# Per-head products over 64 array rows, with the two heads taken in turn, in a two-layer RWKV-7 / gated-unit trunk

## The chip, the cores and the metric

The program runs on one core of a Trainium2 chip. The core has a matrix engine with a 128 by 128 array (TensorE, PE in the profile; PEld is its weight load), a vector engine (VectorE, DVE), a scalar engine (ScalarE, ACT), GpSimd (POOL) and a queue that issues DMAs (SyncE, SP). Each engine runs its own instructions in the order in which the program holds them and waits on semaphores for the others. The metric is device time of one execution, in microseconds.

## The reference, cut to what matters

The trunk has two layers on 512 tokens of width 1024, and a dense feed-forward part behind each layer. The change touches only the token mixer of layer 0, which carries a state per head (16 heads of 64 channels) through time:

```python
def step(S, inp):
    r_t, w_t, k_t, v_t, a_t, b_t = inp
    sa = jnp.einsum('bhij,bhj->bhi', S, a_t)
    S = (S * w_t[:, :, None, :]
         + sa[..., None] * b_t[:, :, None, :]
         + v_t[..., None] * k_t[:, :, None, :])
    y = jnp.einsum('bhij,bhj->bhi', S, r_t)
    return S, y
```

The kernel does not step through time. It cuts the 512 tokens into 8 chunks of 64. Inside a chunk the recurrence becomes a small triangular system per head, so that each chunk and head needs products of keys with queries (64 by 64 blocks), the inverse of a unit triangular matrix, and products with that inverse. Between chunks only the 64 by 64 state is carried.

## The kernel before, in words

The 16 heads are worked in four blocks of four heads (b = 0 to 3). A block holds two pairs of heads (q = 0, 1), and a pair lies on the 128 partitions: the first head on partitions 0 to 63, the second on 64 to 127. For a block the program has these stages:

- `early`: the projections' results become decays, keys and queries, which are written to DRAM in the layout of the next stage (`sa`, `sb`).
- `front`: loads them back and makes the products of keys with queries. It goes over four units: half of the chunks (`hh`, four chunks each) times pair (`q`). For each unit and each head it fills a PSUM bank `lm` with four products, one per chunk (`cc`), at L709. VectorE multiplies one half of the bank by the causal mask and puts it into `MV` (L712), and ScalarE copies other parts into `LA` and `BX` (L715, L716). Four transposes `bkt` (L722) and their copies end the unit. GpSimd masks one part of `BX` at L717.
- `back`: turns `LA` into the inverse. VectorE eliminates 16 by 16 blocks in 15 steps (`tm`, `Dm`, L744 and L746) between 32 by 32 transposes (`LX`, `hn`, `Dt`), and TensorE joins the blocks (`Qp`, `Np`, `Tp`, `Q2p`, `T2p`), with copies into `bdT` (L783, L802). Then for each unit: `mp` (L807, the inverse times a transposed part of `MV`), a copy, and for each head a bank `gh` with four products (L814), from which VectorE makes the final `MV` with two additions (L816, L817).
- `scan`: runs through the eight chunks with the products `us` (next state) and `Yp` (output), then group norm and gating follow.

`MV` holds for each unit and head a 128-partition slab: the head's own queries in its own 64 partitions. The other 64 partitions are zeroed by GpSimd first (L688), because the `lm` product contracts over all 128 partitions while the weights `ST` hold both heads; later the masked product is written to those other partitions. So an `lm` product contracts over 128 rows, 64 of which multiply zeros. A `gh` product already contracts over one head's 64 partitions (`rows`). All these operands are float32, and each such product stands in the profile as two instructions: a bank of four products is eight rows of the trace.

`lm`, `bkt` and `mvt` take PSUM banks 1 and 2 in turn (tag `pl`), and `gh` takes banks 3 and 4 in turn (tag `pt`). The order of the instructions on every engine is set by the framework's scheduler when the program is built: it interleaves the stages of several blocks (the list `PLAN` gives their priority) with the value projection `v`, which is one long run of products over 128 rows, and with the output projection `acc`. After the mixer come output projection, feed-forward, the gated unit of layer 1 and its feed-forward, all outside the change.

## Time and profile before

| | us |
|---|---|
| median of 3 runs (1423.27 to 1425.45) | 1424.7 |
| the profiled execution, its own time | 1426.41 |
| its span, first to last instruction | 1424.7 |
| TensorE busy | 1338.3 (94%) |
| VectorE busy | 791.8 (56%) |
| ScalarE busy | 569.1 (40%) |
| GpSimd busy | 274.5 (19%) |
| mean granted TensorE clock | 0.962 |
| `lm` products, 256 instructions, TensorE busy | 41.6 |
| `gh` products, 256 instructions, TensorE busy | 33.4 |
| zeroing of `MV` on GpSimd, 32 instructions | 16.6 |

The stages around the change lie between 195 us (first `lm`) and 461 us (last `gh`) from the start of the span. Times in rows of the timeline are start and length in microseconds; a row with x16 holds sixteen instructions that follow each other, and its length reaches from the start of the first to the end of the last. Matmuls overlap in the array's pipeline, so the pace of a run of them is read from the starts of the rows and not from the length of one. In the table by stretches each engine's figure is its busy time, PEclk the granted clock.

### The profile page before, as it was taken

The page shows a single profiled execution, that of the slowest core. Times are in us where ns is not written, and L with a number is a line of the kernel's source. Part 1 is how long each engine was busy: PE and PEld are TensorE (multiplying, and loading weights), DVE is VectorE, ACT ScalarE, POOL GpSimd, SP SyncE. Part 2 cuts the span into 40 slices and gives each one's busy share as a digit, 9 for nine tenths or more (in the row PEclk, how much of TensorE's full clock was granted, in tenths as well). Part 3 has the DMA queues.
Part 4 walks back from the last instruction along what each step waited for, and adds up shares of the span by engine and source line. Part 5 has one row for each costly group of instructions (what it writes and reads, how often), then busy time and mean ns, then how long its engine had stood idle before and what let it go on. Part 6 is the DMA issues. An engine that isn't in the chain of part 4 may idle for free.

```text
span 1424.7 us, 21481 instructions
## 1 busy us (share of the span) xinstructions
PE 1338.3 (94%) x8472; PEld 1091.2 (77%) x8472; DVE 791.8 (56%) x1318; ACT 569.1 (40%) x1060; POOL 274.5 (19%) x248
## 2 busy tenths in 40 slices
PE   5899997987889979999999999999999999999998
PEld 3576686976768768888888888778888888888886
DVE  6962776388685775554544222865575455443223
ACT  5654665363723363323322122743363232322221
POOL 6154463133311231111111000210121111110000
PEclk9999998987969989999999999999999999999999
DMA  5133467351322423333332232343213333332331
GB/s 157 30 107 92 127 182 200 94 150 43 87 65 88 130 90 104 89 89 103 90 99 94 89 118 74 104 129 109 89 52 112 103 89 89 103 90 103 89 96 67
DMA packets 210324, 143.04 MB, mean 100 GB/s; under 512 B 59664, under 2 KB 185136, under 8 KB 210224
## 3 DMA queue, kind: packets, MB, share of 16 engines
q1 hardware_dynamic: 208544, 135.90, 32.2%
q0 software_dynamic: 1680, 5.77, 1.3%
q8 instruction: 67, 1.10, 0.3%
q14 instruction: 33, 0.27, 0.1%
HBM read 125.39 MB, written 14.16 MB: 98 GB/s over the span
## 4 chain that ended last, share of the span: by engine, by line
PE 77%; DVE 7%; ACT 2%; issue 2%; DMA 2%; POOL 1%; SPq 1%; DVEq 0%; POOLq 0%; ACTq 0%
PE gu L158 12%; PE gu L156 12%; PE gu L157 12%; PE acc L156 8%; PE acc L157 8%; PE acc L158 8%; PE gh L814 2%; PE lm L709 2%; PE u L156 1%; PE u L158 1%; PE u L157 1%; PE Yp L856 1%; PE mp L807 1%; PE proj L158 1%; PE proj L156 1%
## 5 line engine op out<-in xcount | busy, mean ns | idle before, releaser
L131 ACT CAST whi<-wraw 128x1024 fp32r<-128x1024 f32 x161 | 168.8, 1050 | 472.5 <-PE gu L157 257.2
L132 DVE TENSOR_TENSOR wlo<-wraw,whi 128x1024 fp32r<-128x1024 f32 x161 | 246.6, 1532 | 197.2 <-ACT whi L131 193.2
L157 PE MATMUL gu<-hT,whi 128*128 128x512 f32 (+1 forms) x768 | 289.6, 378 | 4.4 <-DVE hT L59 4.4
L156 PE MATMUL gu<-hT,whi 128*128 128x512 f32 (+1 forms) x768 | 290.2, 380 | 0.8 <-ACT hT L57 0.8
L158 PE MATMUL gu<-hT,wlo 128*128 128x512 f32 (+1 forms) x768 | 289.7, 378 | 0.0
L157 PEld LDWEIGHTS gu<-hT,whi 128*128 128x128 f32 x768 | 146.0, 190 | 34.0 <-DVE hT L59 4.7
L156 PEld LDWEIGHTS gu<-hT,whi 128*128 128x128 f32 x768 | 145.8, 191 | 29.5 <-ACT hT L57 1.0
L158 PEld LDWEIGHTS gu<-hT,wlo 128*128 128x128 f32 x768 | 145.8, 190 | 29.0 <-issue 0.2
L157 PE MATMUL acc<-wlo,act 128*128 128x512 f32 x416 | 163.9, 394 | 0.0
L156 PE MATMUL acc<-whi,act 128*128 128x512 f32 x416 | 163.6, 394 | 0.0
L158 PE MATMUL acc<-whi,act 128*128 128x512 f32 x416 | 160.5, 394 | 0.0
L333 POOL TENSOR_TENSOR sg<-sg,hn 128x512 f32<-128x512 f32 x44 | 56.7, 1288 | 422.5 <-DVE sg L332 422.5
L332 DVE TENSOR_TENSOR sg<-sg,gu 128x512 f32<-128x512 f32 x44 | 30.2, 687 | 142.5 <-PE gu L158 141.1
L148 POOL TENSOR_TENSOR wlo<-wraw,whi 128x1024 fp32r<-128x1024 f32 x28 | 70.1, 2505 | 169.9 <-ACT whi L147 151.1
L158 PEld LDWEIGHTS acc<-whi,act 128*128 128x128 f32 x416 | 78.2, 188 | 18.1
L156 PEld LDWEIGHTS acc<-whi,act 128*128 128x128 f32 x416 | 78.2, 188 | 18.0
L157 PEld LDWEIGHTS acc<-wlo,act 128*128 128x128 f32 x416 | 78.1, 188 | 18.0
L330 DVE TENSOR_TENSOR sg<-gu,hn 128x512 f32<-128x512 f32 x44 | 30.4, 691 | 67.8 <-PE gu L158 67.6
L131 ACT CAST act<-sg 128x512 fp32r<-128x512 f32 x52 | 32.3, 622 | 72.2 <-POOL sg L333 58.1
L158 PE MATMUL proj<-xsp,wlo 128*128 128x512 f32 x128 | 53.7, 421 | 0.0
L156 PE MATMUL proj<-xsp,whi 128*128 128x512 f32 x128 | 51.9, 405 | 0.4 <-ACT k L529 0.4
L709 PE MATMUL lm<-MV,ST 128*128 128x128 f32 x256 | 41.6, 316 | 11.2 <-DMA ST<-sb 7.9
(305 smaller groups left out, 2248.8 us busy)
## 6 DMA issues: line engine op xcount, KB each, us to landing
wraw<-in_ffn_w_gate_dram SPq DMA_DIRECT2D x44, 512.0 KB, 3.6
wraw<-in_ffn_w_up_dram SPq DMA_DIRECT2D x44, 512.0 KB
wraw<-in_ffn_w_down_dram SPq DMA_DIRECT2D x44, 512.0 KB, 3.6
wraw<-in_rwkv_w_rkv_dram SPq DMA_DIRECT2D x24, 512.0 KB, 3.5
wraw<-in_sgu_w_in_dram SPq DMA_DIRECT2D x16, 512.0 KB, 3.6
x<-in_x_dram SPq DMA_DIRECT2D x8, 512.0 KB, 3.7
MV<-sa SPq DMA_DIRECT2D x64, 64.0 KB, 2.6
ST<-sb SPq DMA_DIRECT2D x8, 512.0 KB, 4.5
```

Source lines behind the costliest of these rows:

```text
L131: self.nc.scalar.copy(hi, src)
L132: self.nc.vector.tensor_tensor(lo, src, hi.bitcast(F32), op=ALU.subtract)
L148: nc.gpsimd.tensor_tensor(lo, raw, hi.bitcast(F32), op=ALU.subtract)
L156: mm(out, lhs[0], rhs[0], start=start, stop=False)
L157: mm(out, lhs[0], rhs[1], start=False, stop=False)
L158: mm(out, lhs[1], rhs[0], start=False, stop=stop)
L330: nc.vector.tensor_tensor(sg, pp[0], yb, op=ALU.mult)
L332: nc.vector.tensor_tensor(sg, sg, pp[1], op=ALU.mult)
L333: nc.gpsimd.tensor_tensor(sg, sg, yb, op=ALU.mult)
L709: mm(lm[:, cc * P:(cc + 1) * P], st[:, cc].rearrange("p n t -> p (n t)"), mv[:, :, cc, hd, :], start=True, stop=True)
L807: mm(mp[:, cc * P:(cc + 1) * P], bdT[:, q * NC + 4 * hh + cc].rearrange("p h t -> p (h t)"), mt[:, cc, :], start=True, stop=True)
L814: mm(gh[:, cc * P:(cc + 1) * P], mt[rows, cc, :], bx[rows, 0:2, cc, :], start=True, stop=True)
```

## The change

The zeroing of the other 64 partitions goes. The `lm` product now takes weights and moving operand from one head's 64 partitions only, as `gh` did before. In the text of the program the loops are turned round: two banks are taken at once, one for each head, and for each chunk the two heads' products follow each other, so that neighbouring products use the array's rows 0 to 63 and 64 to 127 in turn. The same turn is made for `gh`. What is read out of the banks, by whom and in which order of heads, is as before.

```diff
                         mv = MV[hh, q] = s4("MV", [P, 2, 4, 2, C])
                         for hd in range(2):
-                            g.memset(mv[head[1 - hd], :, :, hd], 0.0)
                             for n in range(2):
...
+                    lms = [self.bank("pl", "lm") for _ in range(2)]
+                    for cc in range(4):
+                        for hd in range(2):
+                            mm(lms[hd][:, cc * P:(cc + 1) * P], st[head[hd], cc].rearrange("p n t -> p (n t)"),
+                               mv[head[hd], :, cc, hd, :], start=True, stop=True)
                     for hd in range(2):
                         rows, other = head[hd], head[1 - hd]
-                        lm = self.bank("pl", "lm")
-                        for cc in range(4):
-                            mm(lm[:, cc * P:(cc + 1) * P], st[:, cc].rearrange("p n t -> p (n t)"), mv[:, :, cc, hd, :], start=True, stop=True)
-                        lv = lm.rearrange("p (c a t) -> p c a t", c=4, a=2)
+                        lv = lms[hd].rearrange("p (c a t) -> p c a t", c=4, a=2)
...
+                    ghs = [self.bank("pt", "gh") for _ in range(2)]
+                    for cc in range(4):
+                        for hd in range(2):
+                            mm(ghs[hd][:, cc * P:(cc + 1) * P], mt[head[hd], cc, :], bx[head[hd], 0:2, cc, :], start=True, stop=True)
                     for hd in range(2):
-                        rows, other = head[hd], head[1 - hd]
-                        gh = self.bank("pt", "gh")
-                        for cc in range(4):
-                            mm(gh[:, cc * P:(cc + 1) * P], mt[rows, cc, :], bx[rows, 0:2, cc, :], start=True, stop=True)
-                        gv = gh.rearrange("p (c a t) -> p a c t", c=4, a=2)
+                        gv = ghs[hd].rearrange("p (c a t) -> p a c t", c=4, a=2)
```

The scheduler builds its order anew, and its order is what the engines run. Three places follow. First TensorE in `back` of block 3, at the unit whose bank pair is shown (in the changed kernel `us` is L845, `Yp` L858, `gh` L815, `mp` L809). Before, with the second unit:

```order
L807 MATMUL mp_4530<-MVt_4241,bdT_151 128x128 x4
L856 MATMUL Yp_4703<-su_4692,MV_3207 64x64 x2
L856 MATMUL Yp_4703<-su_4692,MV_3214 64x64 x2
L843 MATMUL us_4798<-su_4790,MV_3476 64x64 x2
L814 MATMUL gh_4536<-BX_3543,MVt_4241 128x128 x4
L814 MATMUL gh_4543<-BX_3543,MVt_4241 128x128 x4
L807 MATMUL mp_4550<-MVt_4254,bdT_151 128x128 x4
```

Changed, the same unit:

```order
L809 MATMUL mp_4498<-MVt_4209,bdT_151 128x128 x4
L858 MATMUL Yp_4671<-su_4660,MV_3187 64x64 x2
L858 MATMUL Yp_4671<-su_4660,MV_3192 64x64 x2
L845 MATMUL us_4766<-su_4758,MV_3452 64x64 x2
L815 MATMUL gh_4504<-BX_3511,MVt_4209 128x128
L815 MATMUL gh_4505<-BX_3511,MVt_4209 128x128
L815 MATMUL gh_4504<-BX_3511,MVt_4209 128x128
```

The two heads' banks (4504 and 4505) are filled in turn. Over all four blocks 10 of the 16 `gh` units stand so in the changed program, 2 still have four products of one head directly followed by four of the other, and 4 have other products between the two heads; before, it was 0, 13 and 3.

Second, TensorE at the end of `front` of block 0 and the beginning of `front` of block 1 (`v` is the value projection). Before:

```order
L722 MATMUL bkt_1598<-ident_79,ST_1492 128x128 x4
L709 MATMUL lm_1610<-MV_1501,ST_1492 128x128 x4
L709 MATMUL lm_1619<-MV_1501,ST_1492 128x128 x4
L722 MATMUL bkt_1629<-ident_79,ST_1492 128x128 x4
L757 MATMUL mvt_1691<-ident_79,MV_1478 128x128 x4
L757 MATMUL mvt_1697<-ident_79,MV_1485 128x128 x4
L757 MATMUL mvt_1704<-ident_79,MV_1494 128x128 x4
L757 MATMUL mvt_1710<-ident_79,MV_1501 128x128 x4
L709 MATMUL lm_2080<-MV_2041,ST_2039 128x128 x4
L709 MATMUL lm_2089<-MV_2041,ST_2039 128x128 x4
L722 MATMUL bkt_2099<-ident_79,ST_2039 128x128 x4
L709 MATMUL lm_2111<-MV_2048,ST_2039 128x128 x4
```

Changed:

```order
L724 MATMUL bkt_1590<-ident_79,ST_1488 128x128 x4
L708 MATMUL lm_1602<-MV_1495,ST_1488 128x128 x4
L708 MATMUL lm_1603<-MV_1495,ST_1488 128x128 x4
L724 MATMUL bkt_1621<-ident_79,ST_1488 128x128 x4
L759 MATMUL mvt_1683<-ident_79,MV_1478 128x128 x4
L759 MATMUL mvt_1689<-ident_79,MV_1483 128x128 x4
L759 MATMUL mvt_1696<-ident_79,MV_1490 128x128 x4
L759 MATMUL mvt_1702<-ident_79,MV_1495 128x128 x4
L156 MATMUL v_2417<-whi_2421,xsp_1431 128x256
L156 MATMUL v_2418<-whi_2421,xsp_1431 128x256
L708 MATMUL lm_2064<-MV_2033,ST_2031 128x128 x4
L708 MATMUL lm_2065<-MV_2033,ST_2031 128x128 x4
```

Here the heads are not taken in turn: bank 1602 gets its four products, then 1603 its four. Of the 16 `lm` units one is fully in turn (the last of block 2), one in part (the first of block 0), 5 have the second half of one head's products directly ahead of the other's, and 9 have other products between the two heads. After the last row shown, 27 products of `v` follow in the changed program before `bkt` and the first head of block 1's second unit, 19 more before its second head, and 29 more before `Qp`; before, the two `lm` units of block 1 stood together and 60 of `v` behind them.

Third, VectorE where block 1's last copy into `bdT` stands among the first steps of block 2's elimination (`Y<-Y` is group norm of block 0; in the changed kernel `tm` is L746, `Dm` L748, the copy L804). Before:

```order
L744 TENSOR_TENSOR tm<-LX,Dm 128x2x48
L885 TENSOR_TENSOR Y<-Y,nr_y 128x1024
L746 TENSOR_TENSOR Dm<-Dm,tm 128x2x12x4
L744 TENSOR_TENSOR tm<-LX,Dm 128x2x55
L746 TENSOR_TENSOR Dm<-Dm,tm 128x2x11x5
L802 COPY bdT<-T2p 32x16x32
```

Changed:

```order
L887 TENSOR_TENSOR Y<-Y,nr_y 128x1024
L714 TENSOR_TENSOR MV<-lm,mk_126 64x4x2x64 x2
L737 STREAM_TRANSPOSE LX<-LA 128x1024
L903 TENSOR_TENSOR Y<-Y,hn 128x1024
L746 TENSOR_TENSOR tm<-LX,Dm 128x2x15
L804 COPY bdT<-T2p 32x16x32
```

The copy, for which `mp` of block 1 waits, has moved from behind the fifth step of block 2's elimination to ahead of the end of its first.

## The prediction

> **What bounds the kernel now.** I read the page first, engine shares and chain, then the stretch of the mixer by windows, then the two groups of products, then single rows of the timeline.

> ```profile
> PE 1338.3 (94%) x8472; PEld 1091.2 (77%) x8472; DVE 791.8 (56%) x1318; ACT 569.1 (40%) x1060; POOL 274.5 (19%) x248
> PE 77%; DVE 7%; ACT 2%; issue 2%; DMA 2%; POOL 1%; SPq 1%; DVEq 0%; POOLq 0%; ACTq 0%
> PE gu L158 12%; PE gu L156 12%; PE gu L157 12%; PE acc L156 8%; PE acc L157 8%; PE acc L158 8%; PE gh L814 2%; PE lm L709 2%; PE u L156 1%; PE u L158 1%; PE u L157 1%; PE Yp L856 1%; PE mp L807 1%; PE proj L158 1%; PE proj L156 1%
> ```

> TensorE carries 77% of the chain that ends last, and `gh` and `lm` 2% each, some 28 us apiece. That share is an average over stages with different limits. The windows cut it (columns: length, busy PE, PEld, DVE, ACT and POOL with instruction counts, granted clock, DMA share, GB/s):

> ```profile
> 195.00:240.00 45.00, 35.03 (x258) 31.48 (x259) 28.96 (x48) 29.25 (x67) 23.55 (x29) 0.86 0.72 188
> 240.00:300.00 60.00, 58.30 (x904) 54.51 (x903) 34.13 (x65) 28.68 (x66) 10.71 (x17) 0.96 0.42 119
> 300.00:345.00 45.00, 31.56 (x600) 27.80 (x601) 37.13 (x76) 21.46 (x60) 16.46 (x20) 0.72 0.30 80
> 345.00:380.00 35.00, 33.98 (x592) 28.68 (x591) 19.45 (x45) 19.88 (x59) 5.45 (x11) 0.97 0.28 67
> 380.00:415.00 35.00, 23.97 (x233) 19.76 (x223) 34.50 (x68) 13.81 (x25) 13.45 (x8) 0.62 0.28 93
> 415.00:440.00 25.00, 23.18 (x516) 19.52 (x516) 10.01 (x23) 10.20 (x25) 0.00 (x0) 0.92 0.18 54
> 440.00:490.00 50.00, 49.49 (x454) 40.46 (x453) 38.33 (x89) 17.87 (x43) 16.24 (x16) 1.00 0.42 131
> ```

> TensorE is full in 240 to 300, 345 to 380 and 440 to 490: there less TensorE work is less time. In 300 to 345 and 380 to 415 VectorE is the busy one (37.1 of 45, 34.5 of 35) and TensorE idles at a low clock, and in 195 to 240 TensorE idles 10 us. The long waits of TensorE between 190 and 490 (total, times, longest):

> ```profile
> PE mp L807 <- DVE bdT L802: 12.8, 3, 7.3
> PE lm L709 <- DMA ST<-sb: 7.9, 2, 4.6
> ```

> **What two halves of the array do at once.** First the two groups (busy us, mean ns of one, idle before), then single runs of them:

> ```profile
> L709 PE MATMUL lm<-MV,ST 128*128 128x128 f32 x256 | 41.6, 316 | 11.2 <-DMA ST<-sb 7.9
> L814 PE MATMUL gh<-BX,MVt 64*128 64x128 f32 x256 | 33.4, 313 | 1.8 <-ACT MVt L809 1.1 <-DVE MV L817 0.7
> ```

> Sixteen instructions are one unit, both heads; eight are one head. At full clock, then at half clock:

> ```profile
> 296.81 2.05 PE L709 MATMUL lm<-MV,ST 128*128 128x128 f32 x16
> 286.35 1.16 PE L709 MATMUL lm<-MV,ST 128*128 128x128 f32 x8
> 287.44 1.71 PE L814 MATMUL gh<-BX,MVt 64*128 64x128 f32 x16
> 456.22 1.16 PE L814 MATMUL gh<-BX,MVt 64*128 64x128 f32 x8
> 232.09 3.76 PE L709 MATMUL lm<-MV,ST 128*128 128x128 f32 x16 [4.63 <-DMA ST<-sb]
> 341.15 3.10 PE L814 MATMUL gh<-BX,MVt 64*128 64x128 f32 x16
> ```

> One head takes 1.16 us over 64 rows as over 128, so halving the rows alone buys nothing. Two heads take 2.05 over 128 rows (0.89 more, 8 steps of 0.11) but 1.71 in `gh`, where they lie on different halves, though one head's eight stand wholly ahead of the other's. So 0.34 us, three steps, already overlap at the change of head. Three windows inside one such unit show it (the count is of instructions that run in the window):

> ```profile
> 269.48:270.02 0.55, 0.54 (x4) 1.00 0.00 0
> 270.02:270.47 0.45, 0.45 (x9) 1.00 0.00 0
> ```

> Twice as many run in the second, shorter window, in which the first head ends and the second begins. Heads in strict turn should then take one head's time, 1.16.

> [...]

> **The change, part by part.** *`gh`.* The new order takes 10 of 16 units in turn: 1.71 becomes 1.16, 0.55 saved, about 1.0 at half clock (3.10 to some 2.1). By blocks: block 0 all four, 2.2 us, in the full stretch 240 to 300. Block 1 three, one of them at half clock, 2.1; between them TensorE also waits for the copy of `mp` and for the additions, so I count half, 1.0. Block 2 one at half clock, 1.0, in the stretch that VectorE fills: 0. Block 3 two, 1.1, but one unit's heads, together before, are now apart, which costs (2 x 1.16 - 1.71) 0.6: 0.5 in a full stretch. Sum 3.7 us on the path, of about 6 on the engine. Bounds: 6 saved; or, if alternate products did not overlap, these ten would cost as `lm` does, 10 x 0.34 = 3.4 slower. The second window makes me take the saving.

> *`lm`.* Only one unit is fully in turn (0.89 saved), five stand head behind head (0.34 each, 1.7), nine have other work between and save nothing. Against that, a product over 64 rows among full ones is a change of the array's shape. The price, from `mp` with the same shape behind it and with another:

> ```profile
> 290.74 1.06 PE L807 MATMUL mp<-MVt,bdT 128*128 128x128 f32 x8
> 291.63 0.60 PE L757 MATMUL mvt<-ident,MV 128*128 128x128 f32 x4
> 450.82 1.16 PE L807 MATMUL mp<-MVt,bdT 128*128 128x128 f32 x8
> 451.91 0.45 PE L856 MATMUL Yp<-su,MV 128*64 128x64 f32 x4
> ```

> Start to start it is 0.89 against 1.09, so 0.1 for each change. In the new order 25 sides of `lm` runs newly border on full products (`v`, `ssp`, `bkt`, `yt`, `mp`), 19 of them before 250 us: 2.5 us in all. So on the engine `lm` is nearly even (2.6 saved, 2.5 paid). What is paid early (1.9 against 0.7 saved there) lies in the stretch with 10 us of idle TensorE, 0; without that cover it would cost 1.2. Later 1.9 is saved, 0.6 paid: 1.3 on the path. Bounds: 14 saved (16 x 0.89) if the hardware brought all heads together; 2.5 lost if none overlap.

> [...]

> *The zeroing.* 32 instructions leave GpSimd:

> ```profile
> L688 POOL MEMSET MV<- 64x512 f32 x32 | 16.6, 520 | 27.6 <-DVE MV L816 20.4 <-PE v L158 3.5 <-PE Yp L856 2.2
> ```

> 16.6 us of an engine that is busy 19% of the span; behind them in its queue stand the masks of `BX` and the memsets of the next stage. The loads of `MV` wait in any case for the slot, and the first `lm` for `ST`'s DMA (7.9 above). I count 0; at most the 3.8 us that weight loads of `lm` waited on these memsets, if the DMA were not as late:

> ```profile
> L709 PEld LDWEIGHTS lm<-MV,ST 128*128 128x128 f32 x256 | 36.6, 221 | 14.5 <-issue 9.2 <-POOL MV L688 3.8 <-POOL hn L899 0.4
> ```

> *Both banks at once.* A unit's first head is now read out only when all eight of its turns are done, 1.16 against 1.16 where they run together, so nothing; where a unit is split over other work, the order shows one head first as before.

> *The new order elsewhere.* Products of `v` move from behind block 1's second `lm` unit into its first idle, and `mp` of block 1 gets its last copy earlier. It can give back at most the waits above (12.8 + 7.9) and can make as many new ones. I take 0 and put both signs into the rivals.

> Sum: 3.7 + 1.3 = 5.0 us. From the profiled span, 1424.7, to 1419.7; the span's 1424.7 is also the median of the runs (the profiled execution as a whole took 1426.4, 1.7 around the span), so I predict 1420 for the median.

> **The rivals.** *More than the sum: the wait of `mp` goes.* In block 1:

> ```profile
> 326.22 1.92 DVE L735 STREAM_TRANSPOSE LX<-LA 128x1024 f32<-128x1024 f32 x1
> 336.68 0.69 DVE L802 COPY bdT<-T2p 32x512 f32<-32x512 f32 x1
> ```

> 10.5 us lie between them; in the new order one group-norm product and one step do, about 3.5, then `T2p` sets the time. If 5 of these 7 us arrive at the scan, 1415. Against it: VectorE has the same total work in 300 to 345, so what is pulled ahead delays block 2's elimination.

> *Slower: block 0's inverse comes late.* Place: `Qp` of block 0, at 249 us now. The first `lm` unit of block 1 waits for its DMA until 232 as today and takes up to 3.1 at half clock; 27 products of `v` at 0.12 (0.24 at half clock), then the unit's heads with 19 and 29 more between and behind. Pace of `v`:

> ```profile
> 204.37 0.28 PE L156 MATMUL v<-whi,xsp 128*128 128x256 f32 x1
> 204.49 0.28 PE L157 MATMUL v<-wlo,xsp 128*128 128x256 f32 x1
> ```

> 232.1 + 3.1 + 3.2 to 6.5 + about 1 for transposes and head + 2.3 + 1 + 3.5 puts `Qp` between 246 and 250.5, and VectorE's elimination waits for the mask of that unit's first head in its own queue. With the shape changes ahead of it (1.9) that is up to 3 us late. If VectorE, which fills 37 of the 45 us behind, passes the delay on and the `gh` savings fall into waits, 1424.7 + 3 = 1428. It decides from a `Qp` later than 250.

> *No change.* VectorE sets the pace in 300 to 345 and 380 to 415, and the savings ahead of each are waited away; or shape changes cost more than 0.1: 1423 to 1426.

> [...]

> **How the numbers follow.** The forecast, 1417 to 1422, 0.37; the earlier copy, 1412 to 1416, 0.15; full overlap 0.05; no change 0.23; slower 0.20. About 0.2% (2.9 us) is what a measurement of this kernel can tell from no change. Faster by more is 0.34 of the forecast's 0.37, and 0.15 and 0.05: 0.54. Within it the 0.23 and the forecast's last 0.03: 0.26. Slower 0.20. The range runs from the earlier copy with all 6 us of `gh` (1424.7 - 6 - 1.3 - 7, about 1410) to the late `Qp` with a microsecond for its own uncertainty, 1429.

> **What would show it.** `gh` units in turn should take 1.16 with 16 instructions, and `lm` head behind head 1.71; the group `lm` should fall from 41.6 by 2 to 3 us at most, `gh` from 33.4 by about 6. `Qp` of block 0 should start within a microsecond or two of 249. The stretches 240 to 300 and 440 to 490 should be shorter by 2 and 0.5. I am wrong if alternate `gh` takes 2.05, or if the last `gh` (460 us) comes more than 10 us earlier or any later.

## The result: slower by 1.2%

The changed kernel takes 1437.74 us in the median of 4 runs (1437.46 to 1449.61), the kernel before 1423.99 on the same chip (4 runs, 1419.73 to 1425.45). The ratio is 1.0119, 95% interval 1.0077 to 1.0162: 13.7 us slower, where 1420 was predicted and 1429 was the upper end of the range. The profiled execution of the changed kernel took 1437.75 us, its span is 1436.0; the profiled execution of the kernel before has a span of 1424.7, so the two that are compared below lie 11.3 us apart.

The page of the changed kernel, engine shares and chain:

```profile
PE 1344.0 (94%) x8472; PEld 1090.3 (76%) x8472; DVE 794.1 (55%) x1318; ACT 569.3 (40%) x1060; POOL 257.8 (18%) x216
PE 77%; DVE 7%; DMA 2%; issue 2%; ACT 2%; SPq 1%; POOL 1%; DVEq 0%; POOLq 0%; ACTq 0%
```

Nothing stands out there. The groups of the two products (busy us, mean ns of one, idle before) show that the products got shorter:

```profile
L708 PE MATMUL lm<-MV,ST 64*128 64x128 f32 x256 | 37.9, 322 | 5.5 <-DMA ST<-sb 2.9 <-ACT BX L718 1.7 <-issue 0.6
L815 PE MATMUL gh<-BX,MVt 64*128 64x128 f32 x256 | 29.0, 313 | 3.8 <-ACT MVt L811 1.9 <-DVE MV L819 1.8
```

Two single units in the timeline (start, length):

```profile
286.10 1.16 PE L815 MATMUL gh<-BX,MVt 64*128 64x128 f32 x16
287.10 1.61 PE L708 MATMUL lm<-MV,ST 64*128 64x128 f32 x16
```

`lm` fell from 41.6 to 37.9 us and `gh` from 33.4 to 29.0; a `gh` unit in turn takes 1.16, and an `lm` unit with one head behind the other 1.61. 8.1 us of products are gone, and TensorE is busy 5.7 us longer, so products run longer somewhere. The stretches say where (length, busy PE, PEld, DVE, ACT, POOL with counts, granted clock, DMA share, GB/s):

```profile
345.00:380.00 35.00, 32.29 (x574) 27.04 (x570) 22.17 (x52) 20.51 (x60) 3.31 (x6) 1.00 0.28 66
380.00:415.00 35.00, 17.43 (x222) 14.48 (x223) 32.68 (x63) 10.59 (x18) 11.67 (x7) 0.60 0.29 88
415.00:440.00 25.00, 25.00 (x261) 21.00 (x260) 8.02 (x20) 7.62 (x18) 0.00 (x0) 0.67 0.18 58
```

From 415 to 440 TensorE is busy all the time and gets through 261 instructions, where it got through 516 before: the clock is 0.67 in place of 0.92. Starts (and ends where named) on TensorE, from the timelines, in us:

| | before | changed | difference |
|---|---|---|---|
| `Qp` block 0 | 249.4 | 251.0 | +1.6 |
| `T2p` block 0 | 260.7 | 267.9 | +7.2 |
| `Qp` block 2 | 360.3 | 359.9 | -0.4 |
| `T2p` block 2 | 388.5 | 394.6 | +6.1 |
| first `mp` block 2 | 397.0 | 401.7 | +4.7 |
| `Qp` block 3 | 424.9 | 435.2 | +10.3 |
| end of the last `gh` | 461.5 | 472.2 | +10.7 |
| end of the mixer's last `acc` | 510.2 | 521.7 | +11.5 |

The 7 us that block 0 loses are back by 360 us. Nearly all of the loss, 10.3 of 11.3 us, is there by 435 us, and it arises in block 2, from 376 us on, in two steps.

**First step, 376 to 402.** ScalarE now holds block 1's group-norm square (L883), and then the cast of an output weight that waits for its DMA (L131), ahead of copies of block 2's `MVt` (L762). Before, three of the four copies stood ahead of the square (the first of them at 382.56 us). Timelines of ScalarE (start, length, and in brackets the wait ahead with what ended it), before, then changed:

```profile
384.25 1.07 ACT L760 COPY MVt<-mvt 128x512 f32<-128x512 f32 x2
385.25 1.06 ACT L881 ACTIVATE hn<-Y 128x1024 f32<-128x1024 f32 x1
```

```profile
385.61 1.06 ACT L883 ACTIVATE hn<-Y 128x1024 f32<-128x1024 f32 x1 [3.79 <-DVE Dm L748]
386.57 0.57 ACT L762 COPY MVt<-mvt 128x512 f32<-128x512 f32 x1
388.94 1.04 ACT L131 CAST whi<-wraw 128x1024 fp32r<-128x1024 f32 x1 [1.80 <-DMA wraw<-in_rwkv_w_o_dram]
389.89 0.58 ACT L762 COPY MVt<-mvt 128x512 f32<-128x512 f32 x1
```

The waits of TensorE from 376 to 441 (total, times, longest), the second being the next step's:

```profile
PE mvt L759 <- ACT MVt L762: 4.8, 2, 3.6
PE us L845 <- issue: 3.9, 1, 3.9
```

The square waits 3.8 us for a subtraction on VectorE, and the copies wait behind it. TensorE's next transposes `mvt` need the bank that those copies free, and `Q2p` and `T2p` stand behind them.

**Second step, 402 to 435.** On VectorE the additions that read block 2's first `gh` unit stand behind both transposes of block 3. Changed, then before:

```profile
408.28 1.94 DVE L751 STREAM_TRANSPOSE hn<-Dm 128x1024 f32<-128x1024 f32 x1
410.12 1.88 DVE L752 STREAM_TRANSPOSE Dt<-Dm 128x1024 f32<-128x1024 f32 x1
412.02 0.43 DVE L818 TENSOR_TENSOR MV<-gh,BX 128x256 f32<-128x256 f32 x1
```

```profile
403.87 0.42 DVE L816 TENSOR_TENSOR MV<-gh,BX 128x256 f32<-128x256 f32 x1
...
410.55 2.06 DVE L749 STREAM_TRANSPOSE hn<-Dm 128x1024 f32<-128x1024 f32 x1
```

So the scan's first `us`, which reads `MV`, waits 3.93 us, and TensorE with it. The profile names no releaser for this wait ("issue"); but the first addition ends at 412.45 and `us` starts at 412.55, and in e2, e4 and e7 below the two lie 0.1 us apart as well.

```profile
408.02 0.60 PE L929 MATMUL yt<-ident,Y 128*128 128x128 f32 x4
412.55 0.45 PE L845 MATMUL us<-su,MV 128*64 128x64 f32 x2 [3.93 <-issue]
```

In the windows below the granted clock changes only at edges that lie 3.41 us apart. The same stretch cut at these edges, changed kernel:

```profile
407.66:411.07 3.41, 0.96 (x9) 0.72 (x7) 3.41 (x3) 0.59 (x1) 0.00 (x0) 1.00 0.43 115
411.07:414.48 3.41, 1.93 (x10) 1.75 (x11) 3.38 (x7) 0.62 (x1) 0.00 (x0) 0.50 0.11 41
414.48:417.90 3.42, 3.42 (x15) 2.97 (x15) 0.92 (x3) 0.14 (x1) 0.00 (x0) 0.50 0.20 77
417.90:421.31 3.41, 3.41 (x12) 2.63 (x11) 0.76 (x2) 1.99 (x4) 0.00 (x0) 0.50 0.00 0
...
428.14:431.55 3.41, 3.41 (x18) 2.79 (x17) 1.45 (x3) 0.15 (x1) 0.00 (x0) 0.50 0.02 5
431.55:434.96 3.41, 3.41 (x38) 2.77 (x35) 2.03 (x6) 2.06 (x5) 0.00 (x0) 1.00 0.30 98
```

After a window with 0.96 us of work the clock halves, and then four windows in a row, all of them fully busy (414.5 to 428.1), do not bring it back; behind the fifth it is full, from 431.55 on. That was the riddle. What runs in the four is `gh` one head at a time, on 64 of the 128 rows, with `mp` or a gate between; in the fifth, from 428.45 on, there are transposes over all 128 rows.

### The profile page after: what moved, and what is told of

Same layout as the page of the kernel before. It is cut to its first block, busy times and chain, and to the rows that moved or that the text cites. A ratio compares the mean times of both kernels' runs of the same rounds, so it can differ in the third digit from the quotient of the medians.

```text
span 1436.0 us, 21405 instructions
## 1 busy us (share of the span) xinstructions
PE 1344.0 (94%) x8472; PEld 1090.3 (76%) x8472; DVE 794.1 (55%) x1318; ACT 569.3 (40%) x1060; POOL 257.8 (18%) x216
## 4 chain that ended last, share of the span: by engine, by line
PE 77%; DVE 7%; DMA 2%; issue 2%; ACT 2%; SPq 1%; POOL 1%; DVEq 0%; POOLq 0%; ACTq 0%
PE gu L158 11%; PE gu L157 11%; PE gu L156 11%; PE acc L156 8%; PE acc L157 8%; PE acc L158 8%; PE gh L815 2%; PE lm L708 1%; PE mp L809 1%; PE u L158 1%; PE u L157 1%; PE u L156 1%; PE Yp L858 1%; PE v L156 1%; PE v L157 1%
## 5 line engine op out<-in xcount | busy, mean ns | idle before, releaser
L131 ACT CAST whi<-wraw 128x1024 fp32r<-128x1024 f32 x161 | 168.9, 1049 | 463.5 <-PE gu L157 257.8
L157 PE MATMUL gu<-hT,whi 128*128 128x512 f32 (+1 forms) x768 | 289.7, 378 | 4.4 <-DVE hT L59 4.4
L156 PE MATMUL gu<-hT,whi 128*128 128x512 f32 (+1 forms) x768 | 289.4, 379 | 0.1
L158 PE MATMUL gu<-hT,wlo 128*128 128x512 f32 (+1 forms) x768 | 289.3, 378 | 0.0
L157 PEld LDWEIGHTS gu<-hT,whi 128*128 128x128 f32 x768 | 145.3, 189 | 34.1 <-DVE hT L59 4.7
L156 PEld LDWEIGHTS gu<-hT,whi 128*128 128x128 f32 x768 | 145.0, 190 | 29.5 <-ACT hT L57 0.5
L158 PEld LDWEIGHTS gu<-hT,wlo 128*128 128x128 f32 x768 | 145.3, 189 | 28.9 <-issue 0.2
L157 PE MATMUL acc<-wlo,act 128*128 128x512 f32 x416 | 163.9, 394 | 0.0
L156 PE MATMUL acc<-whi,act 128*128 128x512 f32 x416 | 163.5, 394 | 0.0
L158 PE MATMUL acc<-whi,act 128*128 128x512 f32 x416 | 160.4, 394 | 0.0
L156 PEld LDWEIGHTS acc<-whi,act 128*128 128x128 f32 x416 | 78.2, 188 | 18.1
L158 PEld LDWEIGHTS acc<-whi,act 128*128 128x128 f32 x416 | 78.2, 188 | 18.0
L157 PEld LDWEIGHTS acc<-wlo,act 128*128 128x128 f32 x416 | 78.1, 188 | 18.0
L330 DVE TENSOR_TENSOR sg<-gu,hn 128x512 f32<-128x512 f32 x44 | 30.4, 691 | 68.0 <-PE gu L158 67.8
L131 ACT CAST act<-sg 128x512 fp32r<-128x512 f32 x52 | 32.3, 621 | 72.2 <-POOL sg L333 58.0
L158 PE MATMUL proj<-xsp,wlo 128*128 128x512 f32 x128 | 53.7, 421 | 0.0
L156 PE MATMUL proj<-xsp,whi 128*128 128x512 f32 x128 | 51.8, 404 | 0.5 <-ACT k L529 0.5
L157 PE MATMUL proj<-xsp,whi 128*128 128x512 f32 x128 | 50.7, 400 | 0.9 <-DVE xsp L132 0.9
```

The source lines that it names most:

```text
L131: self.nc.scalar.copy(hi, src)
L156: mm(out, lhs[0], rhs[0], start=start, stop=False)
L157: mm(out, lhs[0], rhs[1], start=False, stop=False)
L158: mm(out, lhs[1], rhs[0], start=False, stop=stop)
L330: nc.vector.tensor_tensor(sg, pp[0], yb, op=ALU.mult)
```

## The experiments

Theory A: the order on ScalarE and VectorE around block 2 is the loss, and not the products. Theory D, formed from the windows above: the clock follows how much of the array works, not whether TensorE is busy. An order is imposed by one call, which adds no wait:

```python
def behind(tc, later, earlier):
    tc.add_manual_dep(later.ins, earlier.ins.name,
                      mybir.DependencyInfo(mybir.DependencyClass.NoSync, mybir.DependencyReason.DATA), reason="order")
```

| run | median us (lowest to highest) | ratio to before, 95% interval |
|---|---|---|
| e1_gh_only | 1423.6 (1421.7 to 1427.1) | 0.9993 (0.9980 to 1.0005) |
| e2_lm_only | 1441.4 (1438.2 to 1442.0) | 1.0111 (1.0090 to 1.0132) |
| e3_add_first | 1433.3 (1431.5 to 1436.8) | 1.0060 (1.0042 to 1.0078) |
| e4_before_add_late | 1437.8 (1434.0 to 1442.1) | 1.0089 (1.0068 to 1.0111) |
| e6_queues | 1434.1 (1427.5 to 1444.6) | 1.0077 (1.0041 to 1.0112) |
| e7_zero_back | 1437.5 (1435.4 to 1453.0) | 1.0120 (1.0071 to 1.0168) |
| e8_gh_turn | 1421.7 (1417.8 to 1426.3) | 0.9985 (0.9965 to 1.0005) |
| e9_turn_b2 | 1441.3 (1432.2 to 1449.5) | 1.0117 (1.0075 to 1.0160) |
| e10_turn_all | 1430.7 (1423.3 to 1437.1) | 1.0041 (1.0021 to 1.0060) |
| e11_turn_all_queues | 1432.1 (1421.2 to 1436.5) | 1.0039 (1.0018 to 1.0060) |
| e12_before_warm | 1426.3 (1423.1 to 1429.8) | 1.0012 (1.0001 to 1.0023) |
| e13_turn_warm | 1420.6 (1416.3 to 1424.6) | 0.9975 (0.9962 to 0.9987) |
| e16_turn_warm_yt | 1420.4 (1416.3 to 1423.1) | 0.9966 (0.9952 to 0.9981) |
| e17_before_warm_yt | 1425.4 (1421.5 to 1429.7) | 0.9999 (0.9985 to 1.0013) |

### Which half of the change, and the zeroing

e1 takes the change of `gh` alone, e2 that of `lm` alone (with the zeroing out), and e7 puts the zeroing back into the changed kernel:

```diff
                         for hd in range(2):
+                            g.memset(mv[head[1 - hd], :, :, hd], 0.0)
                             for n in range(2):
```

> The kernel before with the change in gh alone (heads in turn, both banks taken ahead); lm over 128 rows and the zeroing as before. Theory A (the loss is the order on VectorE and ScalarE around block 2: additions to MV of block 2's first unit stand behind the transposes of block 3, TensorE runs dry for 4 us and its clock falls to half for 20 us): in this build those additions stand ahead of the transposes as before, so no such gap, gh units in turn take 1.16, and the span falls by 2 to 6 us against before. Theory B (heads in turn cost at the read-out, since both banks end together and the first head's addition comes later): 8 us or more slower than before, as the whole change.

> The kernel before with the change in lm alone (64 rows, heads alternating in the source, zeroing left out); gh as before. Theory A: the build has around block 2 the same order on VectorE as the whole change, additions behind the transposes, so 8 to 14 us slower than before, with TensorE dry near 410 us and at half clock until about 430. Theory B (gh in turn is what costs): within 3 us of before.

> The changed kernel with the 32 zeroing instructions put back, so that only the products differ from the kernel before. Its build has VectorE's order around block 2 as the changed kernel has it. Theory A: as slow as the changed kernel, 1434 to 1441. Rival G (without the zeroing GpSimd or the loads of MV come at another time, and that is the loss): back at 1424 to 1428.

e2 is as slow as the whole change, though it leaves `gh` as it was and makes `lm` faster: its build has the whole change's order on VectorE around block 2, and its scan waits there too (2.25 us ahead of `us` at 417.6). e7 has that order as well and is as slow (1437.5). e1's build keeps the additions ahead, and it loses nothing, so reading the banks a little later costs nothing: theory B falls. With the zeroing back the time is the same, so theory G falls with e7. That the change of `lm` turned the order, and neither `gh` nor the missing zeroing, follows from e1, e2 and e7 together.

But e1 was expected 2 to 6 us faster and is not faster. It was 4.1 us ahead at `T2p` of block 3 (436.5 against 440.6) and only 0.8 at the last `gh` (460.7). In block 3 three of its four units stand with the heads apart, TensorE ran short for a moment, and the clock fell:

```profile
450.77:454.18 3.41, 2.76 (x22) 2.25 (x21) 3.27 (x11) 1.10 (x3) 1.30 (x1) 1.00 0.39 139
454.18:457.59 3.41, 3.41 (x11) 2.70 (x11) 2.94 (x9) 0.00 (x0) 0.00 (x1) 0.50 0.08 18
```

### The order alone

e3 is the changed kernel, e4 the kernel before; each adds one order for four additions on VectorE to the source and nothing else. The scheduler then builds anew, and other things move with it:

```diff
+            for n in range(4):                                  # e3
+                behind(tc, ops[3]["step"], ops[2]["add"][n])
+            for n in range(4):                                  # e4
+                behind(tc, ops[2]["add"][n], ops[3]["dt"])
```

> The changed kernel with one order added and nothing else: the four additions of block 2's first gh unit stand ahead of the last step of block 3's elimination on VectorE, and so ahead of the two transposes. Theory A: TensorE's gap of 3.9 us at 408 to 412 goes, the clock is back at full by about 415, 8 to 12 us are won: 1426 to 1430. Rival C (the lateness of T2p and mp of block 2, 6 us at 395, which comes from ScalarE's order, sets the time, and the additions only wait for what is late anyway): 3 us won at most, 1434 or more.

> The kernel before with one order added and nothing else: the four additions of block 2's first gh unit stand behind the second transpose of block 3 on VectorE, as they do in the changed kernel. Theory A: TensorE runs dry ahead of the scan of block 2, the clock stays at half some 15 to 20 us longer, and the kernel is 7 to 13 us slower, 1431 to 1437. Rival C: within 3 us of before, since the additions have slack.

e4 makes the old kernel 12.7 us slower (1437.8 against 1425.1), without one product altered. That it comes out just as slow as the change is partly chance. It lacks the first step (`T2p` of block 2 comes 28.1 us after `Qp`, before 28.2, changed 34.7), and its wait ahead of `us` is 2.0 us, half of the changed kernel's. Its build also put two units of `mp` ahead of the scan and set the two heads of two `gh` units apart, and from 414 to 441 us its clock is at half:

```profile
411.13 1.16 PE L808 MATMUL mp<-MVt,bdT 128*128 128x128 f32 x8 [0.73 <-ACT MVt L810]
414.30 0.44 PE L844 MATMUL us<-su,MV 128*64 128x64 f32 x2 [2.01 <-issue]
```

So the 12.7 us are the price of the order together with what the scheduler moved behind it, not of the additions' place alone. e3 takes 4.4 us off the changed kernel, less than the 8 to 12 expected: TensorE no longer waits at 408, but its clock, full from 409, falls once more at 416 and is back only at 426 (the mean of 415 to 440 us is 0.79, before 0.92). Rival C's 3 us is passed, yet 8 us to the kernel before remain, with `T2p` at 394.3 still late.

> The changed kernel with the order of the run e3_add_first and, on ScalarE, the copies of block 2's transposed MV (MVt) and of Tp ahead of the squares of block 1's group norm and ahead of the cast of the output projection's second weight, as they stand before the change. Theory A (the rest of the loss, 8 us after e3, is ScalarE's order, which makes T2p of block 2 start at 394.5 in place of 388.5): T2p of block 2 comes at 389 to 391, and the kernel takes 1423 to 1428. Rival F (the rest is the block 0 and 1 part, that is the extra shape changes of lm): no more than 2 us better than e3's 1433.

e6 adds to e3 three orders on ScalarE and one for the weight's cast:

```diff
+            for n in range(3):
+                behind(tc, ops[1]["sq"], ops[2]["mvt"][n])
...
+            for c in ops[2]["mvt"] + [ops[2]["tp", 32], ops[2]["tp", 96]]:
+                behind(tc, self.casts[n0 + 4], c)
```

Its eight executions lie at 1427 to 1429 (three), 1434 to 1435 (three) and 1444 to 1445 (two), and its profile is one of the last kind, at a mean clock of 0.941 where e3's has 0.955, so its `T2p` (404.6) can't be put down to the order alone. The three short ones are 3 to 4 us below e3's shortest, as theory A wants; the median is e3's, as the rival F forecast. That ScalarE's order is the first step is therefore argued from the chain above and not shown. e11 below, with e6's orders on ScalarE, has `T2p` of block 2 26.0 us after `Qp`; but e10, without them, has it at 29.2 already, so they do not settle it either.

### What the clock follows

> A program of its own, not the reference's computation: eight stretches of 256 fp32 products with 128 columns each, back to back, with about 14 us of copies on ScalarE between the stretches so that the clock falls. Rows used: all 128 (full); 64, always the same half (half); 64, eight products on one half and then eight on the other (heads); 64 in strict turn (turn); 128 rows but 64 columns of weights (cols); and groups of 128 rows and of 64 rows mixed 3 to 1, 2 to 2 and 1 to 3 (mix3, mix2, mix1). Theory D (what raises the clock is not that TensorE is busy but how much of the array works): full and turn are at full clock within two windows of 3.4 us; half and heads stay at half clock to their end, 55 us in place of 28; the mixed ones show the share from which it rises, by the windows seen so far about 0.77 of the rows, so mix3 (0.875) rises and mix2 (0.75) and mix1 (0.63) do not or late. Rival E (busy is busy): all eight rise within two windows, and 64 rows of one half take the same 0.11 us a product.

In strict order of the stretches: full, half, heads, turn, mix3 (columns as above, the first two figures length and busy PE with the count of products in the window):

```profile
33.98:60.00 26.02, 26.02 (x235) 26.02 (x235) 0.46 (x1) 0.00 (x0) 0.00 (x0) 1.00 0.00 1
64.70:112.00 47.30, 47.30 (x224) 47.30 (x223) 0.00 (x0) 9.78 (x10) 0.00 (x0) 0.50 0.00 1
122.73:136.38 13.65, 13.65 (x200) 13.65 (x198) 0.00 (x0) 6.11 (x6) 0.00 (x0) 1.00 0.01 2
143.21:153.45 10.24, 10.24 (x186) 10.24 (x186) 0.00 (x0) 8.83 (x9) 0.00 (x0) 1.00 0.01 3
191.00:218.00 27.00, 27.00 (x220) 25.31 (x219) 0.00 (x0) 9.78 (x10) 0.00 (x0) 1.00 0.00 1
```

With 64 rows of one half TensorE is busy without a gap for 47 us and is left at half clock. It had come into this stretch at full clock, with 1.7 us of waiting between. Rival E falls. In turn a product takes 0.055 us (10.24 / 186) against 0.111 with all rows (26.02 / 235): two halves at once were twice as fast. This stretch came in with the clock fallen after the pause of 2.0 us ahead of it and had it back after one window, at 143.21 us, which 13 windows of `half` did not do. Where D was wrong is `heads`: eight and eight, they were back at full clock 6.5 us after their start (116.26 to 122.73). In a long run of them every change of half hides about three steps, 0.068 us a product (13.65 / 200) in place of 0.111 over eight, so that much of the time both halves work; that this brought the clock back is D's reading, and was not shown. `cols` (160.28 to 184.00 us) and the mixed stretches (191.0 to 218.0, 228.5 to 252.0, 259.3 to 286.0) kept the full clock, 1.00 in all four, but for one window of a mixed stretch after a pause of 1.7 us. So from which share of rows the clock rises was not found this way, and whether half of the columns count like half of the rows stays open, since `cols` was never at half clock.

> The changed kernel with one order added: in block 2 alone the products of each gh unit stand in strict turn of the heads on TensorE. The additions stay behind the transposes of block 3 and T2p stays late, so the two waits are as in the changed kernel. Theory D (what keeps the clock at half from 411 to 431 us is that the heads of block 2's second and third units stand apart, 64 rows at a time, so that a busy TensorE does not count as busy enough): with the heads in turn the clock is back at full by about 421, two to three windows earlier, and the kernel takes 1429 to 1434. Rival (the idle 4 us alone set it and the recovery takes its time whatever runs): as the changed kernel, 1436 to 1440.

In the kernel itself, e9 changes the order of `gh` in block 2 alone (the scheduler also moved one `mp` unit and the gate there):

```diff
+                            turn.append(mm(ghs[hd][:, cc * P:(cc + 1) * P], mt[head[hd], cc, :], ...))
+                    for later, earlier in zip(turn[1:], turn):
+                        if b == 2:
+                            behind(tc, later, earlier)
```

```profile
408.37:411.78 3.41, 0.74 (x7) 0.51 (x5) 3.41 (x3) 0.58 (x1) 0.00 (x0) 1.00 0.41 154
411.78:415.20 3.42, 2.25 (x10) 1.86 (x11) 3.22 (x7) 0.62 (x1) 0.00 (x0) 0.50 0.01 2
415.20:418.61 3.41, 3.41 (x22) 3.07 (x21) 0.19 (x1) 0.58 (x1) 0.00 (x0) 0.50 0.20 77
418.61:422.02 3.41, 3.41 (x21) 2.50 (x20) 2.29 (x6) 3.00 (x6) 0.00 (x0) 1.00 0.00 0
```

The windows above are e9's. The wait is the same (`us` at 412.9), `T2p` and `mp` are as late (394.9, 402.0), and the clock is back at 418.6 in place of 431.6. `Qp` of block 3 starts at 429.3, 5.9 us earlier. The second step added 5.6 us (from 4.7 to 10.3), so nearly all of it is the time at half clock, and not the wait, which is still there. Of these, 2.0 are left at the end of `acc` (519.7). The median of its six executions is no answer to the question: three took 1432 to 1435, as expected, and three 1448 to 1449.

### Why executions of one program lie 15 us apart

> The kernel of e9_turn_b2 once more, for a second profile: its executions took 1432 to 1435 or 1448 to 1449. If this one is of the long kind, theory D says that a stretch with few rows at work or with a short idle time falls within one 3.4 us window here and across two in the other, so that the clock stays at half for 10 to 30 us longer at one place, and all else is equal; an execution that is longer everywhere, or in its transfers, speaks against it.

e14 caught a long one, 1448.65 us. Up to 355 us the two are alike (end of `mp` in block 1: 355.5 and 355.3). Then TensorE waits for VectorE, for the same time in both. The timeline of e9, then of e14:

```profile
358.16 1.79 PE L816 MATMUL gh<-BX,MVt 64*128 64x128 f32 x16 [1.86 <-DVE MV L824]
```

```profile
357.92 2.39 PE L816 MATMUL gh<-BX,MVt 64*128 64x128 f32 x16 [1.77 <-DVE MV L824]
```

The stretch around it, cut at the clock's steps, and the 20 us behind it, e9, then e14:

```profile
353.76:357.17 3.41, 2.54 (x36) 2.15 (x32) 3.41 (x2) 1.35 (x4) 0.00 (x0) 1.00 0.32 75
357.17:360.58 3.41, 2.42 (x32) 2.33 (x32) 2.96 (x10) 0.60 (x3) 0.00 (x0) 1.00 0.31 72
...
360.00:380.00 20.00, 19.71 (x420) 16.60 (x421) 7.92 (x16) 15.35 (x48) 2.80 (x6) 1.00 0.28 59
```

```profile
355.53:358.94 3.41, 1.64 (x26) 1.53 (x25) 3.11 (x6) 1.05 (x4) 0.00 (x0) 1.00 0.29 68
358.94:362.35 3.41, 3.41 (x72) 3.07 (x70) 1.79 (x5) 1.36 (x6) 0.66 (x1) 0.50 0.33 72
...
360.00:380.00 20.00, 20.00 (x228) 16.59 (x229) 4.99 (x10) 8.23 (x26) 1.84 (x4) 0.50 0.20 44
```

In e9 an edge of the windows cuts the wait of 1.8 us in two, 2.54 and 2.42 us busy, and the clock stays at 1.00. In e14 the wait lies within one window, 1.64 us busy, and the clock halves behind it, until 430.6; what runs meanwhile are mostly 32-row joins, 64-row products and, from 398 us, waits. The difference of 13.8 us in the span is there by 430. Where the edge lies in the program differed between these two executions: at 357.17 us in e9, at 355.53 and 358.94 in e14.

> The kernel of e11_turn_all_queues once more, for a second profile: the profiled execution took 1421, the others up to 1436. Theory D: the 8 to 15 us more of a long execution are one or two further stretches at half clock between 300 and 470 us, with the same instructions in the same order.

e15 took 1434.2 us against e11's 1421.2 profiled. The stretch from 363 to 380 us runs at 0.52 in place of 0.94, and from 364 to 415 us the clock is at half, where e11's is at half from 378 to 409; from 415 to 470 e15's mean clock is 0.88 and e11's 1.00.

### Can both products be taken in turn and be faster?

> The run e1_gh_only with one order added: on TensorE the products of a gh unit stand in strict turn of the heads, so that all 16 units alternate and none has a head apart (other work may stand between). Theory A with D: each unit takes 1.16, the windows in block 3 keep the clock up (e1 fell to half for 3.4 us at 454), and the 4 us that e1 was ahead at 436 stay: 1417 to 1421. Rival H (the end of the mixer is set by the scan of block 3, whatever gh takes): 1422 to 1425 as e1.

> The changed kernel with all 32 units of lm and gh in strict turn of the heads on TensorE (of most units the first product still stands a little ahead, with other work between). This is what the change says it does. Group lm should fall to about 32 us busy or less, gh to about 26. If the order of the other engines were no matter, up to 14 us of lm and 8 of gh would be saved and the time were below 1415; by theory A it depends on where VectorE and ScalarE put block 2's copies and additions: here the additions stand ahead of the transposes again, but behind all steps of the elimination; 1420 to 1432.

> All units of lm and gh in strict turn, and the orders of the run e6_queues on VectorE and ScalarE (additions of block 2's first unit ahead of the last step and the transposes of block 3, copies of MVt and Tp ahead of the group norm's squares). Theory A with D: both waits and the half clock behind them are gone, 1415 to 1422, faster than before. If it is not faster than 1424, something of the lm change itself (shape changes, or the time from the first to the last product of a head) costs on the path.

e8 is e1 with e9's order in every block; e10 is the changed kernel with that order in `gh` and in `lm`, e11 is e10 with the orders of e6, and e15 is e11 once more. e8 is 2 us faster than e1 and cannot be told from the kernel before; at 1421.7 it just misses its range (1417 to 1421). e10 lies in its range; e11, at 1432.1, misses 1415 to 1422. With `lm` in turn too (e10, e11) `lm` falls to 34.8 and 30.4 us busy and `gh` to 25.2 and 24.4, 15 to 20 us less than before the change, and both are 0.4% slower, with time at half clock. e11's one execution of 1421 shows what it can take with less time at half clock (mean clock 0.959, e15's 0.945). Whether the changes of shape, or each head's later end, also cost on the path was not tested apart.

> The kernel before, with ten products of the identity with MVt (128 rows, 512 columns, overwritten by the real ones) put on TensorE between T2p and the first mp of block 2, where it idles 7.3 us, and with the additions of block 2's first gh unit held ahead of the last step of block 3's elimination on VectorE. The ten products add nothing to the result. Theory D (the clock follows how much of the array worked in the last 3.4 us): the clock does not fall at 391, mp and gh of block 2 take 0.89 and 1.44 in place of 1.8 and 2.9 until 415, and 3 to 8 us of that reach the end: 1416 to 1421. Rival (VectorE, which is busy 34.5 of 35 us in 380 to 415, sets the pace there whatever the clock): within 2 us of before.

> The run e8_gh_turn with the same ten products and the same order of the additions as e12_before_warm. Theory D: 1413 to 1419, faster than before by 0.4% or more. Rival: as e8, 1420 to 1423.

Both get extra products over all rows ahead of block 2's first `mp` (their result is overwritten; `last` is the last product of `T2p`) and e3's order; e12 is otherwise the kernel before, e13 is e8:

```diff
+                    if (hh, q) == units[0]:
+                        for _ in range({2: 10}.get(b, 0)):
+                            behind(tc, mm(mp, self.ident, mt.rearrange("p c f -> p (c f)"), start=True, stop=True), last)
```

e12's clock is full from 390.5 to 404.2, where it was at half from 391.6 on before, and the kernel is not faster (1426.3, where theory D wanted 1416 to 1421). Its build put a transposition that waits for VectorE ahead of `gh`:

```profile
387.87 10.15 PE L809 MATMUL mp<-MVt,ident 128*128 128x512 f32 x20
...
403.43 0.66 PE L931 MATMUL yt<-ident,Y 128*128 128x128 f32 x4 [4.51 <-DVE Y L905]
```

> The run e13_turn_warm with eight products of the identity in place of ten, and with the four transpositions of block 1's Y (yt), which stood ahead of block 2's first gh unit on TensorE and waited 4.5 us there for VectorE's additions to Y (seen in e12_before_warm), put behind that unit. Theory D: the idle 4.5 us and the fall of the clock behind them go; gh of block 2 starts at 395 to 397 in place of 400.7; 1414 to 1419. Rival (VectorE sets the pace of block 2): as e13, 1419 to 1422.

> The kernel before with the same eight products and the same orders as e16_turn_warm_yt; its gh stays head by head. Theory D: gh of block 2 runs at full clock from about 397, 2 to 6 us faster than before, 1418 to 1422; what e16 has over this run is what gh in turn is worth with the clock kept up, by the sum of the trace 4 to 5 us. Rival (VectorE sets the pace): within 2 us of before.

e16 is e13, and e17 is e12, with 8 extra products and the late transposition put behind `gh`:

```diff
+            for t in ops[1]["yt"]:
+                behind(tc, t, ops[2]["gh"])
```

e17 is still no faster than before (0.9999). Its clock is full only until 401.3 us and at half until 415.0; its first `gh` starts at 399.7 (399.8 before), and the transposition still waits 1.6 us for VectorE. What TensorE gains ahead of `gh` it waits away, as the rival says for a stretch that VectorE fills.

e16 differs from e17 in the edit of `gh` alone (one head behind the other in e17, in turn in e16). It is 5.0 us faster than e17 and 0.34% faster than the kernel before, the fastest run with e13 (0.25%). But the two builds differ on every engine after 277 us, so the 5.0 us cannot all be put down to `gh`. The profiled executions lie 9.6 us apart, and e16 leads by 2.4 us at the first `lm` (193.1, e17 195.5), up to which the order is still the same. By `T2p` of block 2 it leads by 7.6 and at the end of `acc` by 8.0. The lead arises in blocks 0 and 1, and not in block 2, for which the extra products were put in. e16's `gh` group:

```profile
L818 PE MATMUL gh<-BX,MVt 64*128 64x128 f32 x256 | 22.8, 306 | 1.2 <-ACT MVt L813 0.7 <-DVE MV L826 0.4
```

10.6 us less than before. e13 (1420.6) and e16 (1420.4) both came out where their rivals had them, and not in the ranges that were expected (1413 to 1419, 1414 to 1419). What separates e13 from e8 (1.1 us in the medians) is within their intervals.

## Why the prediction was wrong, step by step

- **`gh` in turn, 1.16 for 1.71:** right, to the hundredth, and 0.055 us a product in the probe.
- **`gh`, 3.7 us on the path of about 6:** the group fell by 4.4 in place of 6, because two units of block 2 stand with their heads apart at half clock. Its worth on the path was never seen with nothing else moving. The 5.0 us of e16 against e17 lie near the 3.7, which is partly luck, since other things moved too. Alone (e1) it was 4.1 us ahead at `T2p` of block 3 and is given back there, by the clock.
- **`lm`:** the group fell by 3.7, where 2 to 3 was the most expected. The heads behind one another took 1.61 (`lm`) and 1.71 (`gh`), far from twice as fast, so they overlap for a few products at most. The full overlap to which the forecast gives 0.05 no run shows: in its place stand these two times, and 0.068 us a product for groups of eight in a long run (e5), where strict turn took 0.055. A change of shape cost about 0.2 in the probe (27.00 us for 220 products where 26.02 hold 235, two changes in 32 products: (0.123 - 0.111) x 16) and not 0.1, so 5 us for 25 of them. Where they cost on the path no run shows.
- **The zeroing, 0, and both banks at once, 0:** right (e7, e1).
- **"The new order elsewhere ... I take 0":** this is the step that failed. It was bounded by 20.7 us on either side, and the 18.7 us between the sum's 5.0 faster and the 13.7 slower lie inside; but it was put at 0 for want of a place. The two rivals named blocks 0 and 1. Block 2 was looked at only for `gh` ("the stretch that VectorE fills: 0"), though the order of its additions against block 3's transposes could be read from the built program. What the runs show in its place: the new orders on ScalarE and VectorE made TensorE wait 4.8 and 3.9 us and put it at half clock from 411 to 431 us, and `Qp` of block 3 came 10.3 us later. The last `gh` came 10.7 us later, a sign of being wrong that the prediction had named. Putting the additions back took 4.4 us off (e3), and putting them late in the old kernel, with what moved behind them, cost 12.7 (e4).
- **The slower rival, `Qp` of block 0 after 250 us:** it came at 251.0, past the rival's point, and `T2p` 7 us late; and nothing of it was left at 360. So the rival had the side right, and place and mechanism wrong. Its terms add up to 249.5 us at most and not to 250.5, below the point at which it was to decide.
- **What the prediction had no term for:** that after a wait the clock stayed at half while 64-row products ran one head at a time, from 414.5 to 428.1 us in the changed kernel, with `mp` or a gate between, and for 47.3 us on one half alone (e5). The second step added 5.6 us, and with the wait left as it was, e9 got 5.9 back by taking the heads in turn. The rows at half clock were in hand, and were used for durations only.

Open remains how much of the first step is ScalarE's order: e6's short executions point to 3 to 4 us and do not settle it.

## What to carry to other kernels

Where a scheduler sets the order, an edit that saves 8 us of products may also move instructions that it does not touch. Here the order of four additions was worth 4.4 us in one kernel (e3) and, with what moved behind it, 12.7 in the other (e4). Compare the built orders on the engines that are read out next, in every block, before pricing the saving. For products on half of the array's rows near a wait, try both halves in turn: here that had the clock back at 418.6 us (e9) in place of 431.6, and one half alone left it at half for 47.3 us (e5). A difference of 1%, 13.8 us, went here with where the edges of the clock's windows lay against a wait of 1.8 us (e9, e14), so look at the granted clock of several executions before explaining one.
